# First normalization in two token halves instead of four quarters, two-bank PSUM tiles and other operand slots: a hybrid decoder layer on one core

## The chip, the core and the metric

The kernel runs on one core of one Trainium2 chip. The metric is the device time of one execution in microseconds (us); the figure for a kernel is the median of its runs. PE is the matrix engine (PEld its weight loads), DVE the vector engine, ACT the scalar engine, POOL the GpSimd engine, SP the engine whose queue issues the transfers (DMAs).

## What is computed

One layer over 1032 tokens (1024 new ones and 8 samples) of width 1024. Cut to what matters here:

```
mix = concat(o, ys) @ w_out                      # delta-rule heads and S5 heads, one output projection
x = layernorm(DN_ALPHA * x + mix, ln1_g, ln1_b)  # the FIRST normalization, over the 1024 features of a token
h = jnp.square(jax.nn.relu(x @ w_ff1))           # MLP, 4096 hidden columns
x = layernorm(DN_ALPHA * x + h @ w_ff2, ln2_g, ln2_b)
```

All is float32. The kernel keeps that precision on PE by splitting each operand into a high part `hi` and a remainder `lo`; a product is three matmuls, hi·hi, hi·lo and lo·hi.

## The kernel before

Activations lie feature by token: `acc` is eight tiles of 128 features by 1032 tokens. `HN` is 516 tokens, a half; `CH` is 258, a quarter. PE follows program order (a manual schedule); on the other engines the framework orders the instructions. A **step** is the work of one block of 128 input features.

The stage of this change lies between the mixers and the pairs of the MLP. `out2` (L1368) does, in this order:

- It loads eight weight tiles of `w_out` to stay (`resident`, L1361), through a small buffer `wraw`, into slots of the tags L and B.
- `units(c0)` (L1377) is the projection of one quarter: eight output tiles, each 4 steps of three matmuls of 258 columns into a one-bank PSUM tile (`dense_q`, L149, lines 156 to 158), then one DVE addition into `acc` (L1381). There are six such PSUM tiles (`PX`).
- `norm` calls `layer_norm_x1` (L1083) for a quarter, four times. It is a generator: at each `yield` PE is given other work worth so many microseconds of its model (`LW`, in the function `ahead`). The parts are: sums over the eight tiles (L1091 to L1097, DVE and POOL); the mean by a matmul with `onesd` (L1103), copied by ACT (L1105); subtraction (L1110 POOL, L1112 DVE), squares on ACT, their sums (L1118, L1119); the variance by small matmuls (L1124), a power on POOL (L1127); transposes that spread it (L1131); then for each of eight tiles one scaling on DVE (L1134) and `split_b` (L1137): ACT writes `hi` (L1142), DVE writes `lo` (L1148), or ACT writes a copy (L1145) and POOL writes `lo` (L1146).
- `plain(c)` (L1409) is the first MLP product for six tiles of 128 hidden columns, for a quarter of each half (258 tokens each): per tile two weight loads of 128x512 (`load_w`, L116: a transfer, ACT `whi` L113, DVE `wlo` L114; two `wraw`, three `whi`, three `wlo` buffers), then for each half 8 steps of three matmuls, ReLU and square on ACT (L1421, L1422) into one of four `hst` buffers and a store (L1423). The work after the first quarters is interleaved by `norm` and `ahead`.
- `t_forms(acc, c)` (L1151) makes four sums and differences per feature block (`tf`, L1159 to L1165) from both halves of a quarter and splits them; it is called twice, after the fourth norm.

Then `ff1` (L1563) runs ten "pairs" of the MLP in a seven-product scheme (line 1441 is every matmul there), on the operand forms B11, B21, B22 (normalized quarters of features and tokens) and T1 to T4. `ff2` makes the second product; its operand slots are drawn one after another from `RING`. `FORMS` says in which tag (Q, B, C, L, X) each form's slots lie. A slot is 128 x 1032.

Of the kernel before, what the change touches and what calls it, by code (L numbers as in the profile page):

```python
# [38 lines left out]
PX = (6, 2)  # L39
# [11 lines left out]
LW = ((2.5, 8.25, 3.0), (3.0, 8.25, 3.0), (3.0, 8.25, 2.0), (3.0, 12.25, 3.5))  # L51
# [10 lines left out]
class Kernel:  # L62
# [53 lines left out]
    def load_w(self, src, pool=None, raws=None):  # L116
        nc = self.nc
        raw = (raws or self.wp).tile([128, 512], F32, name="wraw", tag="wraw", bufs=3 if raws else 2)
# [964 lines left out]
    def layer_norm_x1(self, acc, c0, n, put, lw):  # L1083
        nc = self.nc
        V, G = nc.vector, nc.gpsimd
        items = [acc[i][:, c0:c0 + n] for i in range(8)]

        def total(a, name):
            s = self.tmp(name, n)
            s2 = self.tmp(name + "b", n)  # L1090
            V.tensor_tensor(s, a[0], a[1], op=OP.add)  # L1091
            G.tensor_tensor(s2, a[2], a[3], op=OP.add)
            V.tensor_tensor(s, s, a[4], op=OP.add)
            V.tensor_tensor(s, s, a[5], op=OP.add)
            G.tensor_tensor(s2, s2, a[6], op=OP.add)
            V.tensor_tensor(s, s, a[7], op=OP.add)
            V.tensor_tensor(s, s, s2, op=OP.add)  # L1097
            return s

        tot = total(items, "lns")  # L1100
# [3 lines left out]
        ms = self.tmp("lnsb", n)  # L1104
        nc.scalar.activation(ms, mean, AF.Copy)  # L1105
        acc2 = [self.tmp("lnq%d" % j, n, bufs=1) for j in range(2)]
        for i in range(8):
            d = items[i]
            if i in LS[0]:
                G.tensor_tensor(d, d, ms, op=OP.subtract)  # L1110
            else:
                V.tensor_tensor(d, d, mean, op=OP.subtract)  # L1112
            if i < 2:
                nc.scalar.activation(acc2[i], d, AF.Square)
            else:
                q = self.tmp("lnsq", n, bufs=3)
                nc.scalar.activation(q, d, AF.Square)
                (G if i in LS[1] else V).tensor_tensor(acc2[i % 2], acc2[i % 2], q, op=OP.add)  # L1118
        V.tensor_tensor(acc2[1], acc2[1], acc2[0], op=OP.add)  # L1119
        yield lw[1]  # L1120
        m = n // 3
        pv = self.psm()[:m, 0:3]
        for j in range(3):
            nc.tensor.matmul(pv[:, j:j + 1], acc2[1][:, m * j:m * j + m], self.onesd[:, 0:1], start=True, stop=True)  # L1124
        rs = self.tmp("lnrs", 3)[:m]
        V.tensor_scalar(rs, pv, 4e-6, None, op0=OP.add)
        G.tensor_tensor(rs, rs, self.mhalf[:m].to_broadcast([m, 3]), op=OP.pow)  # L1127
        yield lw[2]
        rb = self.psm()[:, :n]
        for j in range(3):  # L1130
            nc.tensor.transpose(rb[:, m * j:m * j + m], rs[:, j:j + 1].to_broadcast([m, 128]), self.ident[:m, :m])  # L1131
        for i in range(8):
            x = items[i]
            V.scalar_tensor_tensor(x, x, self.lnp[:, 0, i:i + 1], rb, op0=OP.mult, op1=OP.mult)  # L1134
            self.split_b(x, put[i], self.lnp[:, 1, i:i + 1], i not in LS[2])

    def split_b(self, x, dst, b, pool):  # L1137
# [5 lines left out]
        if pool:  # L1143
            t = self.tmp("lnsq", CH, bufs=3)
# [5 lines left out]
    def t_forms(self, acc, c):  # L1150
        nc = self.nc  # L1151
        V, G = nc.vector, nc.gpsimd
        h = [slice(HN * j + CH * c, HN * j + CH * c + CH) for j in range(2)]
        F = {t: self.form(t, c) for t in ("T1", "T2", "T3", "T4")}
        for i in range(4):
            a11, a12 = acc[i][:, h[0]], acc[i][:, h[1]]
            a21, a22 = acc[4 + i][:, h[0]], acc[4 + i][:, h[1]]
            t = [self.tmp("tf%d" % j, CH, bufs=1) for j in range(4)]
# [7 lines left out]
            self.split_b(t[3], F["T4"][i], None, i in TP[3])  # L1166
# [165 lines left out]
    def form(self, t, c):  # L1332
        s = [self.x1slot("x" + t, FORMS[t][c]) for _ in range(2)]
        seg = lambda j: s[j // 4][:, CH * (j % 4):CH * (j % 4) + CH]
        self.fm[t, c] = [(seg(2 * i), seg(2 * i + 1)) for i in range(4)]
        return self.fm[t, c]
# [24 lines left out]
    def resident(self, src, slots, raws=None):  # L1361
        ws = []
        for n_ in range(8):
            z = slots[n_]
            ws.append([self.load_w(src[n_], pool=(z[:, 0:512], z[:, 512:1024]), raws=raws)])
        return ws

    def out2(self, mixo, acc):  # L1368
# [6 lines left out]
        ws = self.resident(self.a["wout"][0], [self.x1slot("wr", w) for w in "LLLLLLBB"], self.tp)  # L1375

        def units(c0):  # L1377
            for n_ in range(8):
                ps = self.mmps(CH)
                yield from self.dense_q(ws[n_], mixo, c0, CH, ps)  # L1380
                V.tensor_tensor(acc[n_][:, c0:c0 + CH], acc[n_][:, c0:c0 + CH], ps, op=OP.add)  # L1381
                yield 3 * CH / 2400.0

        def norm(c, half, fill):
            put = (self.form("B11", c) + self.form("B21", c)) if not half else (self.form("B12", c) + self.form("B22", c))
            for wait in self.layer_norm_x1(acc, HN * half + CH * c, CH, put, LW[2 * c + half]):
                self.ahead(fill, wait)

        order = [(0, 0), (0, 1), (1, 0), (1, 1)]
# [546 lines left out]
```

## Time and profile before

| | |
|---|---|
| median of 3 runs | 1266.06 us (1263.64 to 1267.84) |
| the profiled execution | 1262.84 us; its span 1260.7 us; 2.1 us lie around the span |
| instructions | 25210 |
| PE busy | 1205.4 us, 96% of the span |
| DVE, ACT, POOL busy | 811.1, 637.3, 497.4 us |
| granted PE clock, mean | 0.982 |
| the stage of the change in the trace | from 491.94 us (first matmul of `out2`) to 630.93 us (first matmul of the pairs) |

Times in the rows are from the span's start. A busy time on PE includes time at a lowered clock. The releaser that a row names is the instruction whose end came last before the waiting one started.

### The profile page before, as it was taken

How to read it: one execution, taken by the hardware profiler on the slowest of the kernel's cores; microseconds unless marked ns; L12 is line 12 of the kernel's file. 1: busy time of each engine (PE TensorE's matmuls, PEld its weight loads, DVE VectorE, ACT ScalarE, POOL GpSimd, SP SyncE). 2: the span in 40 equal slices, each digit the busy share in tenths (PEclk: the TensorE clock that was granted, in tenths of full speed). 3: DMA queues.
4: the chain of work that ended last, by engine and by line, in shares of the span. 5: the costliest groups of instructions: out<-in, count | busy, mean ns of one | idle time of the engine just before them, and what ended most of it. 6: DMA issues, size and time to landing. Idle time of an engine off the chain costs nothing.

```text
span 1260.7 us, 25210 instructions
## 1 busy us (share of the span) xinstructions
PE 1205.4 (96%) x9268; PEld 1177.4 (93%) x9268; DVE 811.1 (64%) x1716; ACT 637.3 (51%) x1450; POOL 497.4 (39%) x533
## 2 busy tenths in 40 slices
PE   8999999899899899989999999999999999999996
PEld 7999999889899899988999999999999999999996
DVE  6476887788636894877745554454566575666667
ACT  5376677663646751357655555555552434352301
POOL 6243333362113660544433233323433636365214
PEclk9999999999979899999999999999999999999999
DMA  7223223122611263013446556545963646453202
GB/s 211 98 81 93 70 70 79 43 51 95 211 56 42 54 195 114 1 52 106 147 173 220 211 194 210 185 177 178 317 199 93 192 124 181 135 174 108 66 35 102
DMA packets 117995, 162.16 MB, mean 129 GB/s; under 512 B 31192, under 2 KB 70632, under 8 KB 117872
## 3 DMA queue, kind: packets, MB, share of 16 engines
q1 hardware_dynamic: 117872, 160.55, 40.5%
q8 instruction: 73, 1.20, 0.4%
q14 instruction: 50, 0.41, 0.1%
HBM read 109.94 MB, written 49.38 MB: 126 GB/s over the span
## 4 chain that ended last, share of the span: by engine, by line
PE 74%; DVE 13%; DMA 5%; ACT 3%; issue 3%; POOL 2%; SPq 0%; POOLq 0%; DVEq 0%; ACTq 0%
PE sb L1441 37%; PE mm L156 7%; PE mm L158 7%; PE mm L157 7%; DMA hst<-ht 1%; PE mm L1741 1%; DMA xraw<-in_xT 1%; DVE xB L1148 1%; DMA hst<-hd 1%; PE mm L1742 1%; PE mm L1743 1%; DVE acc L1134 1%; DVE wlo L114 1%; DMA hraw<-hd 1%; DVE cx L305 1%
## 5 line engine op out<-in xcount | busy, mean ns | idle before, releaser
L114 POOL TENSOR_TENSOR wlo<-wraw,whi 128x512 fp32r<-128x512 f32 (+1 forms) x88 | 109.1, 1241 | 188.6 <-ACT whi L113 167.9
L113 ACT ACTIVATE whi<-wraw 128x512 fp32r<-128x512 f32 (+1 forms) x164 | 100.3, 611 | 146.6 <-PE sb L1441 83.6
L1441 PE MATMUL sb<-t,whi 128*128 128x258 f32 x1008 | 162.5, 284 | 5.5 <-ACT whi L113 3.7
L1441 PEld LDWEIGHTS sb<-t,whi 128*128 128x128 f32 x1008 | 138.6, 190 | 6.7 <-ACT whi L113 4.3
L1441 PE MATMUL sb<-xT,whi 128*128 128x258 f32 x832 | 133.8, 282 | 0.0
L156 PE MATMUL mm<-xhi,whi 128*128 128x344 f32 x384 | 126.1, 328 | 0.9 <-ACT sraw L297 0.5
L157 PE MATMUL mm<-xlo,whi 128*128 128x344 f32 x384 | 123.8, 322 | 0.0
L158 PE MATMUL mm<-xhi,wlo 128*128 128x344 f32 x384 | 123.8, 322 | 0.0
L1695 DVE TENSOR_TENSOR acc<-acc,sb 128x516 f32<-128x516 f32 x112 | 76.5, 688 | 66.5 <-PE sb L1441 66.0
L1441 PEld LDWEIGHTS sb<-xT,whi 128*128 128x128 f32 x832 | 114.0, 189 | 0.0
L1441 PE MATMUL sb<-t,wlo 128*128 128x258 f32 x504 | 100.7, 283 | 0.1
L1441 PE MATMUL sb<-xB,whi 128*128 128x258 f32 x624 | 100.2, 282 | 0.0
L1441 PEld LDWEIGHTS sb<-xB,whi 128*128 128x128 f32 x624 | 85.6, 189 | 0.0
L1441 PE MATMUL sb<-xT,wlo 128*128 128x258 f32 x416 | 83.5, 282 | 0.0
L113 ACT ACTIVATE t<-hst 128x516 fp32r<-128x516 f32 x84 | 52.3, 632 | 51.6 <-DMA hst<-hd 23.9
L1441 PEld LDWEIGHTS sb<-t,wlo 128*128 128x128 f32 x504 | 77.8, 189 | 0.6 <-POOL wlo L114 0.3
L114 DVE TENSOR_TENSOR wlo<-wraw,whi 128x512 fp32r<-128x512 f32 (+1 forms) x76 | 57.1, 752 | 27.4 <-ACT whi L113 26.9
L156 PEld LDWEIGHTS mm<-xhi,whi 128*128 128x128 f32 x384 | 72.3, 188 | 2.2 <-ACT sraw L297 1.1
L157 PEld LDWEIGHTS mm<-xlo,whi 128*128 128x128 f32 x384 | 72.3, 188 | 0.4 <-issue 0.4
L158 PEld LDWEIGHTS mm<-xhi,wlo 128*128 128x128 f32 x384 | 72.2, 188 | 0.4 <-issue 0.4
L1484 DVE TENSOR_TENSOR hst<-sb,hst 128x516 f32<-128x516 f32 x40 | 27.6, 693 | 58.7 <-PE sb L1441 55.1
L114 POOL TENSOR_TENSOR t<-hst,t 128x516 fp32r<-128x516 f32 x36 | 51.4, 1437 | 32.5 <-ACT t L113 30.2
(512 smaller groups left out, 3528.8 us busy)
## 6 DMA issues: line engine op xcount, KB each, us to landing
hd<-hst SPq DMA_DIRECT2D x52, 258.0 KB
wpair<-in_wff SPq DMA_DIRECT2D x26, 512.0 KB
ht<-hsum SPq DMA_DIRECT2D x48, 258.0 KB
hst<-ht SPq DMA_DIRECT2D x48, 258.0 KB
w2raw<-in_wff SPq DMA_DIRECT2D x57, 192.0 KB
wraw<-in_win SPq DMA_DIRECT2D x40, 256.0 KB
hst<-hd SPq DMA_DIRECT2D x36, 258.0 KB
wraw<-in_wff SPq DMA_DIRECT2D x32, 256.0 KB
```

What stands on the lines that cost most here:

```text
L113: nc.scalar.activation(hi, src, AF.Copy)
L114: (lo_eng or nc.vector).tensor_tensor(lo, src, hi.bitcast(F32), op=OP.subtract)
L156: nc.tensor.matmul(ps, hi[:, k % 4, :], mh, start=(k == 0), stop=False)
L157: nc.tensor.matmul(ps, hi[:, k % 4, :], ml, start=False, stop=False)
L158: nc.tensor.matmul(ps, lo[:, k % 4, :], mh, start=False, stop=(k == last))
L305: nc.vector.scalar_tensor_tensor(out, raw[:, j:j + NP], cw[:, t, j:j + 1], out, op0=OP.mult, op1=OP.add)
L1134: V.scalar_tensor_tensor(x, x, self.lnp[:, 0, i:i + 1], rb, op0=OP.mult, op1=OP.mult)
L1148: nc.vector.scalar_tensor_tensor(lo, x, b, hi.bitcast(F32), op0=OP.add, op1=OP.subtract)
L1441: self.nc.tensor.matmul(ps[:, 512 * c:512 * c + CH], a[:, k, :], forms[c][k][b], start=(start and k == 0 and a is hi and b == 0), stop=(st ...
L1484: V.tensor_tensor(h3, self.banks(ps), h3, op=OP.add)
L1695: V.tensor_tensor(a, a, self.banks(ps), op=OP.add)
L1741: nc.tensor.matmul(ps, hi[:, k % 4, :], mh, start=(k == 0), stop=False)
```

## The change

The first normalization works on 516 tokens at a time, two blocks instead of four. The projection and the plain tiles work on halves as well: `units(half)` and `plain(half)` have one two-bank PSUM tile for 516 tokens and `dense_h`, whose step is six matmuls of 258 columns. `PX` becomes three two-bank tiles and one two-bank tile `st`, which serves mean, variance and spread scale of a block in turn. The plain tiles run all of the first half, then all of the second; the weights are still loaded twice. `t_forms` handles 516 tokens, cycles seven temporaries that the normalization used, yields to PE after each feature block, and writes the last two blocks of T4 after the plain tiles. Each form has one slot per feature block that holds `hi` and `lo` of 516 tokens, and `FORMS` and `RING` name other tags in another order. The weights of the projection pass through the temporaries `lnsq`. Cut to the core:

```diff
-RING = "XXLLLLLLQBQBQBQBQBQBQBQQCQCQQB"
+RING = "XXQQQQBBBBBBBBLLLLQQQQQQQQLLCC"
-FORMS = {"B11": "QL", "B21": "QL", "B12": "XX", "B22": "CL", "T1": "BQ", "T2": "BQ", "T3": "BQ", "T4": "BQ"}
+FORMS = {"B11": "BBBB", "B21": "QQQQ", "B12": "CCXX", "B22": "LLLL", "T1": "BBBB", "T2": "QQQQ", "T3": "QQQQ", "T4": "LLCC"}
-PX = (6, 2)
+PX = (3, 1)
-LW = ((2.5, 8.25, 3.0), (3.0, 8.25, 3.0), (3.0, 8.25, 2.0), (3.0, 12.25, 3.5))
+LW = ((3.0, 11.0, 3.0), (3.0, 13.0, 3.5))
+TW = 9.0
+TMPS = ("tf0", "tf1", "lns", "lnq0", "lnq1", "lnsb", "lnsb")
...
+    def layer_norm_half(self, acc, half, put, lw):
+        items = [acc[i][:, HN * half:HN * half + HN] for i in range(8)]
...
         yield lw[0]
-        mean = self.psm()[:, :n]
-        nc.tensor.matmul(mean, self.onesd, tot, start=True, stop=True)
+        st = self.sm.tile([128, 1024], F32, name="st", tag="sm")
+        mean = self.banks(st)
+        for c in range(2):
+            nc.tensor.matmul(mean[:, c, :], self.onesd, s[:, CH * c:CH * c + CH], start=True, stop=True)
...
         yield lw[1]
-        m = n // 3
-        pv = self.psm()[:m, 0:3]
-        for j in range(3):
+        m = CH // 3
+        pv = st[:m, 300:306]
+        for j in range(6):
...
         yield lw[2]
-        rb = self.psm()[:, :n]
-        for j in range(3):
+        for j in range(6):
+            nc.tensor.transpose(mean[:, j // 3, ...], rs[:, j:j + 1].to_broadcast([m, 128]), self.ident[:m, :m])
         for i in range(8):
+            x = self.halves(items[i])
+            V.scalar_tensor_tensor(x, x, self.lnp[:, 0, i:i + 1], mean, op0=OP.mult, op1=OP.mult)
+            self.split_b(items[i], put[i], self.lnp[:, 1, i:i + 1], i not in LS[2])
...
+    def dense_h(self, w, mov, h0, ps):
+        last = 4 * len(w) - 1
+        for k in range(last + 1):
+            hi, lo = w[k // 4]
+            for j, (a, b) in enumerate(((hi, 0), (hi, 1), (lo, 0))):
+                for c in range(2):
+                    self.nc.tensor.matmul(ps[:, 512 * c:512 * c + CH], a[:, k % 4, :],
+                                          mov[k][b][:, h0 + CH * c:h0 + CH * c + CH], ...)
+            if k < last:
+                yield 6 * CH / 2400.0
...
-        order = [(0, 0), (0, 1), (1, 0), (1, 1)]
...
-        norm(1, 1, first)
-        if TO == 2:
-            self.t_forms(acc, 0)
-        self.t_forms(acc, 1)
-        self.ahead(first, 999)
-        self.ahead(self.plain(1), 999)
+        self.ahead(units(0), 99)
+        rest = units(1)
+        norm(0, rest)
+        self.ahead(rest, 99)
+        rest = (x for half in range(2) for x in self.plain(half))
+        norm(1, rest)
+        for wait in self.t_forms(acc):
+            self.ahead(rest, wait)
+        self.ahead(rest, 999)
```

## Rows read from the trace of the kernel before

**Rows 1.** The page of the whole execution: busy time, share of the span and instructions of each engine; then the chain of work that ended last, by engine.

```profile
PE 1205.4 (96%) x9268; PEld 1177.4 (93%) x9268; DVE 811.1 (64%) x1716; ACT 637.3 (51%) x1450; POOL 497.4 (39%) x533
...
PE 74%; DVE 13%; DMA 5%; ACT 3%; issue 3%; POOL 2%; SPq 0%; POOLq 0%; DVEq 0%; ACTq 0%
```

**Rows 2.** Windows: from:to, the length, then busy time and instructions of PE, PEld, DVE, ACT and POOL, the granted PE clock, the DMA share and GB/s.

```profile
491.90:631.10 139.20, 127.65 (x1008) 124.90 (x1007) 106.95 (x210) 74.99 (x191) 63.91 (x75) 0.96 0.23 73
...
542.90:631.10 88.20, 79.01 (x602) 76.55 (x601) 69.33 (x123) 61.85 (x158) 43.68 (x50) 0.94 0.36 112
...
550.00:560.00 10.00, 6.40 (x41) 6.19 (x40) 8.78 (x16) 5.61 (x16) 5.34 (x7) 0.83 0.23 69
...
590.00:600.00 10.00, 7.97 (x51) 7.39 (x50) 9.96 (x17) 8.55 (x22) 6.24 (x7) 0.83 0.16 54
...
620.00:630.00 10.00, 10.00 (x74) 10.00 (x73) 4.39 (x8) 5.49 (x15) 2.56 (x3) 0.83 0.69 210
```

**Rows 3.** Waits of PE: who waited for whom, us in total, times, longest. The first three rows are of the stage (491.9 to 631.1), the last is the largest of the rest of the execution (631.1 to 1260.7).

```profile
PE mm L158 <- DVE wlo L114: 6.6, 4, 3.6
PE mm L157 <- DVE xB L1148: 2.5, 4, 1.8
PE ps L1124 <- DVE lnq L1119: 2.4, 1, 2.4
...
PE sb L1441 <- ACT whi L113: 3.7, 3, 2.0
```

**Rows 4.** PE in order of time: start, duration, line, output and inputs, shape, count, and in brackets the idle time before and its releaser. They are the first matmul of the stage; the mean, the variance and the spread of the first quarter, each with the second matmul behind it; the first plain matmul; the matmul after the longest wait; the first matmul of the pairs.

```profile
491.94 0.28 PE L156 MATMUL mm<-moh,wr 128*128 128x258 f32 x1
...
506.31 0.60 PE L1103 MATMUL ps<-lns,onesd 128*128 128x258 f32 x2
...
506.86 0.28 PE L157 MATMUL mm<-mol,wr 128*128 128x258 f32 x1
...
516.09 0.55 PE L1124 MATMUL ps<-onesd,lnq 128*86 128x1 f32 x6
...
516.70 0.28 PE L157 MATMUL mm<-mol,wr 128*128 128x258 f32 x1
...
520.18 0.39 PE L1131 MATMUL ps<-ident,lnrs 86*128 86x86 f32 x3
...
520.57 0.28 PE L157 MATMUL mm<-mol,wr 128*128 128x258 f32 x1
...
542.92 0.28 PE L156 MATMUL mm<-xB,whi 128*128 128x258 f32 x1
...
555.82 0.41 PE L158 MATMUL mm<-xB,wlo 128*128 128x258 f32 x1 [3.60 <-DVE wlo L114]
...
630.93 0.63 PE L1441 MATMUL sb<-xB,whi 128*128 128x258 f32 x4
```

**Rows 5.** DVE in order of time, columns as in the rows above: the last addition of a projection quarter and the last of its sums; the eight scalings of the first quarter and the first `lo` behind them.

```profile
503.61 0.42 DVE L1381 TENSOR_TENSOR acc<-acc,mm 128x258 f32<-128x258 f32 x1 [1.01 <-PE mm L158]
...
504.60 0.43 DVE L1097 TENSOR_TENSOR lns<-lns,lnsb 128x258 f32<-128x258 f32 x1
...
520.73 3.24 DVE L1134 SCALAR_TENSOR_TENSOR acc<-acc,lnp,ps 128x258 f32<-128x258 f32 x8
523.88 0.98 DVE L1148 SCALAR_TENSOR_TENSOR xB<-acc,lnp,xB 128x258 fp32r<-128x258 f32 x1
```

**Rows 6.** Groups of DVE instructions: line, names, shapes, count, busy us and mean ns of one, idle time before and its releasers. The first is of the page (the same addition on 516 columns, in the second product); the others are of the stage.

```profile
L1695 DVE TENSOR_TENSOR acc<-acc,sb 128x516 f32<-128x516 f32 x112 | 76.5, 688 | 66.5 <-PE sb L1441 66.0
...
L114 DVE TENSOR_TENSOR wlo<-wraw,whi 128x512 fp32r<-128x512 f32 x23 | 20.0, 872 | 10.6 <-ACT whi L113 10.6
L1148 DVE SCALAR_TENSOR_TENSOR xB<-acc,lnp,xB 128x258 fp32r<-128x258 f32 x20 | 15.3, 810 | 0.0
L1381 DVE TENSOR_TENSOR acc<-acc,mm 128x258 f32<-128x258 f32 x32 | 13.3, 418 | 11.9 <-PE mm L158 11.9
...
L1161 DVE TENSOR_TENSOR tf<-acc,tf 128x258 f32<-128x258 f32 x8 | 5.6, 700 | 0.3
L1165 DVE TENSOR_TENSOR tf<-acc,tf 128x258 f32<-128x258 f32 x8 | 5.3, 661 | 0.7 <-POOL xT L114 0.6
L114 DVE TENSOR_TENSOR xT<-tf,xT 128x258 fp32r<-128x258 f32 x10 | 5.0, 518 | 0.5 <-ACT xT L113 0.5
L1159 DVE TENSOR_TENSOR tf<-acc 128x258 f32<-128x258 f32 x8 | 5.0, 622 | 0.6 <-POOL xT L114 0.6
L1148 DVE SCALAR_TENSOR_TENSOR xT<-tf,lnbd,xT 128x258 fp32r<-128x258 f32 x6 | 3.3, 555 | 0.3 <-ACT xT L1142 0.3
```

**Rows 7.** Groups of POOL instructions, columns as in rows 6: two of the normalization and its `lo` at 258 columns, then a subtraction of 516 columns from the second product.

```profile
L1110 POOL TENSOR_TENSOR acc<-acc,lnsb 128x258 f32<-128x258 f32 x16 | 12.5, 815 | 3.9 <-ACT lnsb L1105 3.9
L1146 POOL TENSOR_TENSOR xB<-lnsq,xB 128x258 fp32r<-128x258 f32 x12 | 10.9, 913 | 19.2 <-ACT lnsq L1145 19.1
L1118 POOL TENSOR_TENSOR lnq<-lnq,lnsq 128x258 f32<-128x258 f32 x12 | 10.5, 872 | 3.8 <-ACT lnsq L1117 3.6
...
L114 POOL TENSOR_TENSOR t<-hst,t 128x516 fp32r<-128x516 f32 x36 | 51.4, 1437 | 32.5 <-ACT t L113 30.2 <-PE sb L1441 2.1
```

**Rows 8.** SP's queue in order of time: the first weight transfer after those fetched ahead for the plain tiles, and the first transfer for the pairs.

```profile
555.79 0.33 SPq L119 DMA_DIRECT2D wraw<-in_wff  x1
...
623.53 0.92 SPq L1461 DMA_DIRECT2D wpair<-in_wff  x2
```

More of the change, by code (lines that the diff above doesn't have):

```diff
@@ L1148, in split_b, with t_forms @@
             nc.vector.scalar_tensor_tensor(lo, x, b, hi.bitcast(F32), op0=OP.add, op1=OP.subtract)
-    def t_forms(self, acc, c):
+    def t_forms(self, acc):
         nc = self.nc
         V, G = nc.vector, nc.gpsimd
-        h = [slice(HN * j + CH * c, HN * j + CH * c + CH) for j in range(2)]
-        F = {t: self.form(t, c) for t in ("T1", "T2", "T3", "T4")}
+        F = {t: self.form(t) for t in ("T1", "T2", "T3")}
+        F["T4"] = []
+        h = [slice(HN * j, HN * j + HN) for j in range(2)]
+        last = []
         for i in range(4):
@@ L1165, in t_forms @@
             V.tensor_tensor(t[3], a21, t[1], op=OP.subtract)
[L1166 removed]
+            last.append(t[3])
+            if i < 2:
+                F["T4"].append(self.piece("T4", i))
+                self.split_b(t[3], F["T4"][i], None, i in TP[3])
+            yield TW if i < 3 else 999
+        for i in range(2, 4):
+            F["T4"].append(self.piece("T4", i))
+            self.split_b(last[i], F["T4"][i], None, i in TP[3])
+        self.form_views("T4", F["T4"])
     def weave(self, main, filler, per_us, per_stage=0.0):
@@ L1384, in norm @@
-        def norm(c, half, fill):
-            put = (self.form("B11", c) + self.form("B21", c)) if not half else (self.form("B12", c) + self.form("B22", c))
-            for wait in self.layer_norm_x1(acc, HN * half + CH * c, CH, put, LW[2 * c + half]):
-                self.ahead(fill, wait)
-        order = [(0, 0), (0, 1), (1, 0), (1, 1)]
-        us = [units(HN * half + CH * c) for c, half in order]
-        self.ahead(us[0], 99)
-        chain = lambda *gs: (x for g in gs for x in g)
-        norm(0, 0, chain(us[1], us[2]))
@@ L1394, in out2 @@
-        self.ahead(us[1], 99)
-        norm(0, 1, chain(us[2], us[3]))
-        self.ahead(us[2], 99)
-        if TO == 0:
-            self.t_forms(acc, 0)
-        first = self.plain(0)
-        norm(1, 0, chain(us[3], first))
-        self.ahead(us[3], 99)
-        if TO == 1:
-            self.t_forms(acc, 0)
-        norm(1, 1, first)
-        if TO == 2:
-            self.t_forms(acc, 0)
-        self.t_forms(acc, 1)
-        self.ahead(first, 999)
-        self.ahead(self.plain(1), 999)
@@ L1411, in plain, with norm @@
-    def plain(self, c):
+                ps = self.mmh()
+                yield from self.dense_h(ws[n_], mixo, HN * half, ps)
+                a = self.halves(acc[n_][:, HN * half:HN * half + HN])
+                V.tensor_tensor(a, a, self.banks(ps), op=OP.add)
+                yield 6 * CH / 2400.0
+        def norm(half, fill):
+            put = self.form("B1%d" % (half + 1)) + self.form("B2%d" % (half + 1))
+            for wait in self.layer_norm_half(acc, half, put, LW[half]):
+                self.ahead(fill, wait)
@@ L1412, in plain @@
+        self.ahead(units(0), 99)
[7 more added lines that the diff above has]
+        self.ahead(rest, 999)
+    def plain(self, half):
         nc = self.nc
-        mov = [self.fm["B1%d" % (h + 1), c] + self.fm["B2%d" % (h + 1), c] for h in range(2)]
+        mov = self.fm["B1%d" % (half + 1)] + self.fm["B2%d" % (half + 1)]
@@ L1416, in plain @@
             w = self.load_w8(self.a["wff1"][f])
-            for half in range(2):
-                ps = self.mmps(CH)
-                yield from self.dense_q(w, mov[half], 0, CH, ps)
-                h = self.hst()[:, :CH]
-                nc.scalar.activation(h, ps, AF.Relu)
-                nc.scalar.activation(h, h, AF.Square)
-                nc.sync.dma_start(self.hd[f][:, HN * half + CH * c:HN * half + CH * c + CH], h)
-                yield 3 * CH / 2400.0
+            ps = self.mmh()
+            yield from self.dense_h(w, mov, 0, ps)
+            h = self.hst()
+            nc.scalar.activation(self.halves(h), self.banks(ps), AF.Relu)
+            nc.scalar.activation(h, h, AF.Square)
+            nc.sync.dma_start(self.hd[f][:, HN * half:HN * half + HN], h)
+            yield 6 * CH / 2400.0
     def bank(self):
```

89 lines of the change are left out of this document (45 added, 44 removed).

## The prediction

> **What bounds the kernel now.** The page comes first: PE is busy 96% of the span and makes up 74% of the chain that ended last [rows 1]. A change that leaves PE's work alone can only win back time in which PE waits or runs at a lowered clock, so the next views are PE's waits and the windows. The stage of the change lasts 630.93 - 491.94 = 139.0 us [rows 4]. From its first matmul to the first mean lie 120 matmuls (96 of a quarter and 8 steps of three), so one takes (506.31 - 491.94) / 120 = 0.1198 us [rows 4]; a step of six takes 0.719. The stage has 384 + 576 = 960 of them: 115.0 us. A norm adds 0.43 for the mean, 0.49 for the variance and 0.27 for the spread, each from its start to the second matmul behind it, less one matmul [rows 4]; four norms make 4.8. PE's own work is therefore 119.8 us, and 19.2 us are lost. Of these 11.5 are waits: 6.6 for the weight remainders `wlo`, 2.5 for `lo` parts of the normalized operands, 2.4 for a sum of squares, all of them DVE's [rows 3]. The clock is the next part: three windows of 10 us show 0.83 [rows 2], that is some 3.4 us at 1.2 GHz in place of 2.4, and half of this, 1.7, is lost each time. Each of the three follows a wait, as the longest one of 3.60 us [rows 4]. 2.6 us are left for restarts.
>
> Behind it stands DVE: 106.95 us busy in 139.2, and 69.33 of 88.2 from the first plain matmul on [rows 2], where every wait but one lies. So the question is when DVE's work falls due.
>
> **The change, step by step.** *PE's work* stays: 192 matmuls per half of the projection, 288 per half of the plain tiles, and two norms of 0.86 + 0.98 + 0.54 make the same 4.8 us. Forecast times below count 0.719 a step.
>
> *DVE's price.* The same addition costs 418 ns on 258 columns and 688 on 516 [rows 6], so 258 more columns cost 0.27, and a merged pair saves 0.15 at most; eight scalings in 3.24 us are 0.405 each [rows 5], so 0.675 on 516. A `lo` took 0.81 on average, twice what the scaling of the same form does; POOL works on its own `lo` parts at the time [rows 6, 7]. No row shows 516 columns of it. Below it cannot be cheaper than the scaling, 0.675; above, it waits for one whole POOL instruction, 1.44 on 516 [rows 7], so 2.1. I take the nearest row scaled like the scaling, 0.81 x 0.675 / 0.405 = 1.35.
>
> *First norm.* The first half of the projection ends at 491.94 + 32 x 0.719 = 514.9. Three DVE instructions, in before 1.4 us from the last addition to the last sum's end [rows 5], take 2.2 and end at 517.4; PE asks after 5 steps, at 518.5. After the mean (519.4) seven POOL instructions of 1.44 and about 1.7 for ACT and the last DVE sum make 11.8; PE asks after 18 steps, 12.9 us. Both are covered. The spread is done at 537.4, and 4 of 32 steps remain, until 540.3. Here the cover ends. In the rows eight scalings run first and the `lo` parts behind them [rows 5], so DVE scales until 537.5 + 8 x 0.675 = 542.9 and the first `lo` is there at 544.2. PE has done two matmuls and waits **3.7 us**; before, three quarters were through with their `lo` parts or nearly so when the plain tiles began. The next `lo` parts, one late projection addition (0.69) among them, come at 545.6, 547.6 and 549.0, slower than PE's steps; the lowered clock that I expect after the wait lies inside this pace. The second norm's mean, due after 5 steps at 543.9, is reached at 550.2, and its sum, with two more DVE instructions of about 0.9 behind the fifth `lo` (550.3), is ready at 552.1. Mean at 552.15: **8.25 us late**, all causes together (bounds: 3.8 less with `lo` at 0.675; 3.8 more with 2.1).
>
> *Second norm.* 21 steps, 15.1 us, cover its 11.8; 6 steps cover the power. Spread done at 573.9, with 16 steps of the first half left as cover (11.5 us) for DVE's 5.4 of scalings and 6.75 of `lo`, and with three `wlo` of 0.87 [rows 6] and the first T differences in the same queue. I expect no wait for the `lo` parts but one `wlo` late by 2.0 us (mean of the four before 1.65, longest 3.6 [rows 3]) and a lowered clock after it, 1.7: **3.7 us** (bounds 0 and 5.3).
>
> *Weights.* Before, a plain weight served both halves in turn, and the second weight of the next tile had to be split in the 2.9 us between the release of a `whi` and its need. Now one is used for four steps on end, 2.9 us, and three buffers leave 5.7 us for a split of some 1.5. So the 6.6 us of `wlo` waits go, but for the one above. SP issues half as many stores, of twice the size; the weight transfer that before stood behind a store [rows 8] does so still.
>
> *T forms.* Their DVE groups sum to 24.2 us [rows 6]; at 688 / (2 x 418) per column pair that is 20. Before, the first quarters' T forms ran between the third and fourth norms' work; now all of them come after the second norm, at 579.4. From there DVE has 6.75 + 20 + 14 x 0.87 = 39 us to do in the 44 until the pairs. It fits narrowly, and the pairs' later products want the last T forms later still.
>
> *Start of the pairs.* Their first transfers went out 7.4 us ahead of their first matmul [rows 4, 8], and PE did not wait. Two temporaries of T4's last blocks now stay busy to the end; if they held the room of the first transfer, up to those 7.4 us would come bare. Only two of four buffers are needed first, so I put 0.5, for PSUM banks and T1 too.
>
> *Second product.* The ring has the same 30 slots, each index one slot; the first plain forms now take slots whose last use is the last pair's first or third product, not its fourth. Nothing changes on the path: PE's waits there are small (the largest group 3.7 [rows 3]). I allow 2 us either way for shifted timing.
>
> **Sum.** 573.9 + 64 steps (46.0) + 3.7 + 0.5 = 624.1 against 630.93: 6.8 us less. The profiled execution gives 1262.84 - 6.8 = 1256.0; it is 3.2 below the median of the runs, so the forecast for the median is 1266.06 - 6.8 = **1259.3 us**.
>
> **Rivals.** A, *no late queue*: `lo` at 0.675 (for it: DVE and POOL seldom need the same moment in the longer instructions; against: every norm's rows show the mean of 0.81). Mean at 548.35, 3.8 earlier, and no second wait, another 3.7: 14.3 less, 1251.8 us.
>
> B, *each `lo` is held for a whole POOL instruction*, 2.1 us. The mean of 0.81 at 258 is 0.4 more than the scaling, half of POOL's 0.91 [rows 6, 7], which speaks for half a hold, not a whole one. The second mean comes 3.8 later, the rest as forecast: 3.0 less, 1263.1 us, which is no change that can be told. The Trainium skill ("SBUF — State Buffer", section "Who interferes with whom") says that a DVE instruction with two SBUF inputs and a reading GpSimd instruction exclude each other for the whole instruction; by that rule longer POOL instructions speak against this change. By its rule the sum would be B's 1263.1, by the row 1259.3.
>
> C, *slower: DVE is the bound from the second norm on.* The hold of B also falls on the T forms: (6.75 + 20) x 2.1 / 1.35 + 12.2 = 53.8 us from 579.4, so to 633.2; the last `wlo` lies at the end of that queue with one weight's 2.9 us of PE behind it, less the about 2 us of T work that may follow it: pairs at 634.1, 3.2 later, and 1.0 for T1: 4.2 more, 1270.3 us. It decides from the point at which DVE's work after 579.4 exceeds PE's 44 us. For it: DVE is 9.96 busy of 10 in the window at 590 before [rows 2]. Against it: T forms may run on into the pairs, where DVE has room.
>
> That the edit fails to do what it says can be left out: tile widths and order are fixed in the code.
>
> **How the numbers follow.** Forecast 0.44, A 0.21, B 0.18, C 0.17. About 0.3% (3.8 us) is what a measurement of this kernel can tell from no change: faster means below 1262.3, slower above 1269.9. The forecast's own spread (1255 to 1263, from the second wait's bounds and the 2 us of the second product) lies nearly all in faster, A wholly, a little of B: 0.62. Same takes most of B and a share of C: 0.22. Slower is the rest of C: 0.16. The range leaves out the ends of A and C: 1250 to 1268.5.
>
> **What would show it.** Right: the first plain matmul at about 540, with a wait of 3 to 4 us behind its first two, for `lo`; a second mean at 551 to 553; spread of the second at 573 to 575; `wlo` waits of PE of 3 us at most in place of 6.6; one or two windows at a lowered clock in place of three; DVE up to 9 us less busy in the stage (some 60 merged pairs of 0.15); the pairs at 622 to 626. Wrong, if PE waits for a sum of squares (POOL longer than 1.44 each), if plain matmuls wait for T work or for PSUM evacuation, if the first pair's transfers come after the last plain matmul, or if the time after the first pair differs by more than 2 us.

## The result and the profile after

The changed kernel takes 1273.12 us (median of 6 runs, 1270.45 to 1276.03), the kernel before in the same comparison 1264.04 (6 runs): ratio 1.0085, 95% interval 1.0067 to 1.0104 (the quotient of the two medians is 1.0072). It is slower by 9 us; the forecast was 6.8 us faster. The profiled execution took 1274.95 us (span 1273.2), 12.1 more than that of before. In the experiments below, one run of the changed kernel "without T, `lo` one scaling behind" and one of before beside it lie apart at a far lower granted clock (0.748 and 0.653) and are left out.

First, as for before, the page's busy times of the changed kernel:

```profile
PE 1211.9 (95%) x9268; PEld 1182.9 (93%) x9268; DVE 807.9 (63%) x1625; ACT 625.5 (49%) x1366; POOL 493.3 (39%) x496
```

DVE is less busy than before [rows 1], and 91 instructions fewer. The averages look better and the time is worse. The waits of PE in the stage, 491.69 to 638.86, tell more (who waited for whom: us in total, times, longest):

```profile
PE mm L1363 <- DVE wlo L116: 9.8, 5, 4.9
PE mm L1363 <- DVE xB L1149: 4.5, 2, 3.8
PE sb L1464 <- ACT whi L115: 1.2, 1, 1.2
PE st L1125 <- DVE lnq L1120: 0.9, 1, 0.9
PE mm L1363 <- DVE acc L1390: 0.9, 1, 0.9
```

The stage is 147.2 us, 8.2 longer than before. The `wlo` waits, which the forecast had all but removed, went from 6.6 [rows 3] to 9.8; the `lo` waits from 2.5 to 4.5; those for a sum of squares fell from 2.4 to 0.9. PE in order of time (start, duration, what, and in brackets the idle time before and its releaser): the first variance, the first plain matmuls with the forecast wait, the second mean, the second spread and the matmul behind it, then the `wlo` waits of the first four tiles that had any, and the first pair.

```profile
533.55 1.08 PE L1125 MATMUL st<-onesd,lnq 128*86 128x1 f32 x12 [0.91 <-DVE lnq L1120]
...
543.08 0.41 PE L1363 MATMUL mm<-xB,whi 128*128 128x258 f32 x2
547.25 0.51 PE L1363 MATMUL mm<-xB,whi 128*128 128x258 f32 x2 [3.76 <-DVE xB L1149]
...
554.26 1.46 PE L1104 MATMUL st<-lns,onesd 128*128 128x258 f32 x4
...
576.02 0.61 PE L1131 MATMUL st<-ident,lnrs 86*128 86x86 f32 x6
576.42 0.73 PE L1363 MATMUL mm<-xB,whi 128*128 128x258 f32 x4
...
590.70 0.80 PE L1363 MATMUL mm<-xB,wlo 128*128 128x258 f32 x2 [4.85 <-DVE wlo L116]
596.58 0.51 PE L1363 MATMUL mm<-xB,wlo 128*128 128x258 f32 x2 [0.36 <-DVE wlo L116]
601.23 0.51 PE L1363 MATMUL mm<-xB,wlo 128*128 128x258 f32 x2 [1.49 <-DVE wlo L116]
606.74 0.80 PE L1363 MATMUL mm<-xB,wlo 128*128 128x258 f32 x2 [2.37 <-DVE wlo L116]
...
638.86 0.74 PE L1464 MATMUL sb<-xB,whi 128*128 128x258 f32 x4 [1.21 <-ACT whi L115]
```

The second spread is done at 576.42, when the next matmul starts. That is 84.7 us after the first matmul of the stage, 2.8 us behind the forecast (82.0); from there to the pairs it takes 62.4 against 50.2. So 12.2 of the 15 us lie behind the second norm. What stood in DVE's queue there (same columns; x8 is eight instructions in one row):

```profile
576.66 5.39 DVE L1135 SCALAR_TENSOR_TENSOR acc<-acc,lnp,st 128x516 f32<-128x516 f32 x8 [2.22 <-PE st L1131]
581.97 0.68 DVE L116 TENSOR_TENSOR wlo<-wraw,whi 128x512 fp32r<-128x512 f32 x1
582.57 0.69 DVE L1162 TENSOR_TENSOR tf<-acc 128x516 f32<-128x516 f32 x1
583.18 0.69 DVE L1162 TENSOR_TENSOR lnq<-acc 128x516 f32<-128x516 f32 x1
583.79 5.18 DVE L1149 SCALAR_TENSOR_TENSOR xB<-acc,lnp,xB 128x516 fp32r<-128x516 f32 x3
588.90 1.75 DVE L116 TENSOR_TENSOR wlo<-wraw,whi 128x512 fp32r<-128x512 f32 x1
```

The `whi` of the last row was ready at 580.1 (ACT, 0.61 us from 579.52). Its remainder started 8.8 us later, behind T differences and three `lo` parts of 1.73 us each, and took 1.75 itself. A 516-column instruction is 0.69 here when POOL rests. What POOL did at that time:

```profile
580.21 1.31 POOL L1166 TENSOR_TENSOR lns<-acc 128x516 f32<-128x516 f32 x1 [6.47 <-DVE acc L1135]
582.07 4.66 POOL L1147 TENSOR_TENSOR xB<-lnsq,xB 128x516 fp32r<-128x516 f32 x2 [0.55 <-ACT lnsq L1146]
586.70 1.72 POOL L1166 TENSOR_TENSOR lnsb<-acc 128x516 f32<-128x516 f32 x1
588.38 1.72 POOL L1147 TENSOR_TENSOR xB<-lnsq,xB 128x516 fp32r<-128x516 f32 x1
```

The two take turns: 1.73 on DVE in place of 0.69, 1.72 on POOL in place of 1.31. Windows of 10 us (busy time and count of PE, PEld, DVE, ACT, POOL, then the granted clock):

```profile
530.00:540.00 10.00, 9.09 (x68) 8.88 (x68) 5.11 (x8) 0.00 (x0) 3.68 (x3) 0.83 0.01 2
580.00:590.00 10.00, 5.85 (x49) 5.64 (x47) 10.00 (x11) 7.64 (x14) 9.24 (x5) 0.96 0.08 26
590.00:600.00 10.00, 8.68 (x48) 8.18 (x48) 10.00 (x10) 6.48 (x12) 6.61 (x5) 0.70 0.27 79
600.00:610.00 10.00, 6.41 (x40) 6.20 (x41) 10.00 (x13) 6.89 (x12) 5.59 (x3) 0.83 0.25 81
620.00:630.00 10.00, 10.00 (x86) 10.00 (x85) 2.60 (x4) 4.67 (x8) 0.00 (x0) 1.00 0.48 157
```

DVE is full for 30 us and nearly idle in the window at 620: the T work came in a burst, long before the pairs need it. In and behind the waits the clock is lowered: at 0.96, 0.70 and 0.83 the three windows from 580 on hold 10.2 us at 1.2 GHz. For 2.0 us of them PE was still in a wait (from 589.2 to 590.7 and from 606.2 to 606.7), where the clock costs nothing; the other 8.2 us cost half, 4.1 us. With 46.0 of steps and 9.8 and 1.2 of waits that makes 61.1 of the 62.4; 1.3 are left for PE's restarts behind its waits.

### The profile page after: what moved, and what is told of

Read it like the earlier page. It is cut to its first block, busy times and chain, and to the rows that moved or that the text cites. A ratio compares the mean times of both kernels' runs of the same rounds, so it can differ in the third digit from the quotient of the medians.

```text
span 1273.2 us, 24939 instructions
## 1 busy us (share of the span) xinstructions
PE 1211.9 (95%) x9268; PEld 1182.9 (93%) x9268; DVE 807.9 (63%) x1625; ACT 625.5 (49%) x1366; POOL 493.3 (39%) x496
## 4 chain that ended last, share of the span: by engine, by line
PE 75%; DVE 10%; DMA 5%; issue 4%; ACT 3%; POOL 2%; SPq 1%; POOLq 0%; DVEq 0%; ACTq 0%
PE sb L1464 37%; PE mm L158 6%; PE mm L159 6%; PE mm L160 6%; PE mm L1363 5%; DMA hst<-ht 1%; PE mm L1764 1%; PE mm L1766 1%; PE mm L1765 1%; DMA hraw<-hd 1%; DVE t L116 1%; DVE acc L1135 1%; PE mm L145 1%; DVE xB L1149 1%; PE mm L146 1%
## 5 line engine op out<-in xcount | busy, mean ns | idle before, releaser
L116 DVE TENSOR_TENSOR wlo<-wraw,whi 128x512 fp32r<-128x512 f32 (+1 forms) x76 | 60.4, 796 | 33.8 <-ACT whi L115 31.4
L1363 PE MATMUL mm<-xB,whi 128*128 128x258 f32 x384 | 67.1, 298 | 4.5 <-DVE xB L1149 4.5
```

The lines of the kernel that those rows point to most:

```text
L116: (lo_eng or nc.vector).tensor_tensor(lo, src, hi.bitcast(F32), op=OP.subtract)
L1363: self.nc.tensor.matmul(ps[:, 512 * c:512 * c + CH], a[:, k % 4, :], mov[k][b][:, h0 + CH * c:h0 + CH * c + CH], start=(k == 0 and j == 0) ...
```

## The experiments

"After" is the changed kernel, "before" the former one. Each ratio is against runs of before on the same chip (median 1262.8 to 1263.6). The changed kernel itself ran only in the comparison above, whose interval is 2.3 us to either side; a difference to its 1273.1 is no more exact than that.

| kernel | median us | ratio to before (95%) |
|---|---|---|
| before without T | 1256.65 | 0.9942 (0.9929 to 0.9956) |
| after without T | 1259.64 | 0.9966 (0.9954 to 0.9978) |
| after, T paced | 1266.34 | 1.0021 (1.0007 to 1.0035) |
| after, POOL off | 1265.31 | 1.0015 (1.0001 to 1.0029) |
| after, only the norms' `lo` on DVE | 1272.28 | 1.0079 (1.0055 to 1.0104) |
| after, both cures | 1261.83 | 0.9985 (0.9971 to 0.9998) |
| ... and `lo` one scaling behind | 1259.73 | 0.9967 (0.9952 to 0.9982) |
| ... or one `lo` per two scalings | 1259.76 | 0.9973 (0.9958 to 0.9988) |
| after without T, `lo` one scaling behind | 1255.90 | 0.9946 (0.9929 to 0.9964) |
| before, POOL off | 1268.74 | 1.0039 (1.0024 to 1.0055) |
| before, POOL off, T paced | 1265.01 | 1.0013 (0.9999 to 1.0027) |
| after, all cures, stores on POOL's queue | 1255.94 | 0.9954 (0.9936 to 0.9971) |

My theory was that T work in front of the weight remainders, and instructions held for POOL, make the loss. The rivals: DVE's amount of work; something else in the new layout.

### Without the T forms

The T forms' operands are replaced by those of the plain tiles, in both kernels (the edit of the changed one is shown). This leaves out their work on DVE, ACT and POOL, so the results are not the layer's:

```diff
-        for wait in self.t_forms(acc):
-            self.ahead(rest, wait)
+        for t, b in (("T1", "B11"), ("T2", "B21"), ("T3", "B22"), ("T4", "B11")):
+            self.form_views(t, self.fm[b])
```

> The changed kernel without the T forms (their computation is left out; the pairs read the normalized forms in their place, as many matmuls as before). Theory 'late weights': in the changed kernel all T work falls on DVE and POOL right after the second norm, the weight remainders wait in DVE's queue behind it, and this is where the time went. Then of PE's 9.8 us of waits for wlo some 3 are left (the one behind the second norm's scalings and lo parts), with one stretch at the lower clock fewer or two: 1259 to 1263 us. Rival 'shape': the loss lies in the two-bank tiles, the single tile for the norm and the other slots; it stays without T work: 1270 us or more.

> The kernel before, likewise without the T forms. Late weights: it too loses the waits that T work causes, the one of 2.0 and two of 0.5 us for wlo and a stretch at the lower clock: 1257 to 1261 us, so that the two kernels without T forms stand within 3 us of each other. Shape: the changed one stays 8 us slower than this one.

Before without T came 0.4 us below its range, after within it. Without T the two stand 3.0 us apart, with T 9.1 (1273.1 against 1264.0). So some 6 us of the loss come with the T work and 3 do not. `wlo` waits of after fall from 9.8 to 2.6 and, what I had not expected, those of before from 6.6 [rows 3] to 1.7. T work had made most of them before, too.

### The T work in another order, or without POOL

First, the first and the third difference of each T block are pinned behind what is issued ahead of them on their engine:

```diff
+            pin = self.tc.keep_in_program_order
-            V.tensor_tensor(t[0], a12, a11, op=OP.subtract)
+            pin(V.tensor_tensor(t[0], a12, a11, op=OP.subtract))
...
-            (G if i in TE else V).tensor_tensor(t[2], a22, a12, op=OP.subtract)
+            pin((G if i in TE else V).tensor_tensor(t[2], a22, a12, op=OP.subtract))
```

> The changed kernel, with the first difference (DVE) and the third (POOL) of each feature block of the T forms pinned behind everything issued before them on their engine, so that the four blocks are spread over the plain tiles of the second half and the weight remainders pass between them. Same work. Late weights: PE's waits for wlo fall from 9.8 to 4 to 6 us (the longest, 4.9, lies among the second norm's lo parts and loses only the T differences ahead of it, about 1.3), 1267 to 1270 us. Shape: no change, 1273 us.

6.8 us of the loss came back, a little more than expected, with the same work on the same engines: `wlo` waits 4.5. DVE's busy time in the stage is nearly the same (94.6 us, 95.75 in the changed kernel), so the order alone carries most of it. Then the order is left, and POOL's part of the T forms and of the norms' `lo` goes to DVE:

```diff
-LS = ((1, 3, 4, 7), (2, 4, 6), (0, 1, 2, 3, 6))
+LS = ((1, 3, 4, 7), (2, 4, 6), (0, 1, 2, 3, 4, 5, 6, 7))
...
-TP = ((1, 3), (0, 1, 3), (0,), (2,))
+TP = ((), (), (), ())
...
-TE = (0, 1, 2, 3)
+TE = ()
```

> The changed kernel with all T work and all lo parts of the normalization on DVE, none on POOL (three lo parts per norm and eleven instructions of the T forms move). Theory 'hold': a DVE instruction with two inputs in SBUF costs 1.7 us instead of 0.68 while POOL works, so DVE gets faster by more than the moved work: lo parts at 0.68, the second mean at 551 to 552 instead of 554.3, waits for wlo 4 to 6 us instead of 9.8, 1264 to 1268 us. Rival 'amount': DVE is simply full there, and the 17 moved instructions of 0.6 us add 10 us to it: 1277 us or more.

DVE got 17 instructions more and its busy time in the stage fell from 95.75 to 90.87 us. That is the amount rival's end. (ACT loses ten copies by the edit, too; but the `whi` above was ready 8.8 us ahead of its remainder, so ACT was not what held that one up.) DVE of this kernel in order of time, from the second norm's scalings on:

```profile
574.67 5.39 DVE L1135 SCALAR_TENSOR_TENSOR acc<-acc,lnp,st 128x516 f32<-128x516 f32 x8 [1.88 <-PE st L1131]
579.97 0.68 DVE L116 TENSOR_TENSOR wlo<-wraw,whi 128x512 fp32r<-128x512 f32 x1
580.57 0.69 DVE L1162 TENSOR_TENSOR tf<-acc 128x516 f32<-128x516 f32 x1
581.18 0.69 DVE L1162 TENSOR_TENSOR lnq<-acc 128x516 f32<-128x516 f32 x1
581.79 2.08 DVE L1149 SCALAR_TENSOR_TENSOR xB<-acc,lnp,xB 128x516 fp32r<-128x516 f32 x3
583.79 0.69 DVE L1166 TENSOR_TENSOR lns<-acc 128x516 f32<-128x516 f32 x1
584.39 0.68 DVE L116 TENSOR_TENSOR wlo<-wraw,whi 128x512 fp32r<-128x512 f32 x1
```

It is the same beginning as above, but three `lo` take 2.08 in place of 5.18 and the second `wlo` ends 5.1 us after the first began, not 8.7. To see whether the norms' part or the T forms' part of POOL's work mattered, only `LS` was changed, `TP` and `TE` left:

> The changed kernel with only the norms' three lo parts each moved from GpSimd to DVE; the T forms stay as they are, with their work on both engines. Theory 'the T forms' hold is what costs': the second mean moves from 554.3 to about 552.6, the waits for weight remainders stay at 7 to 10 us, and the time is 1270 to 1273 us, at most 2 to 3 under the changed kernel's 1273.1. Rival 'the norm's lo parts' (most of what the kernel without GpSimd won, 7.8 us, came from them): waits of 5 us, 1265 to 1268.

As the theory had it: second mean at 552.34, `wlo` 9.4, 1272.3. The mean came true by luck: of the 1.9 us by which it comes earlier after the stage's start, 1.5 were won before the first spread, which the edit does not touch (a lowered clock behind the first variance that this execution did not have). The time is 0.8 us under the changed kernel's, which the intervals cannot tell from nothing. So POOL's `lo` parts of the norms cost little, and that its T work cost the other 7 follows by subtraction; it was not tried alone. Now both cures, pinned order and POOL off:

> The changed kernel with both cures at once: GpSimd does none of the lo parts and differences of the norm's last step and of the T forms, and the first and third difference of each T block are pinned behind what is issued before them on their engine. Alone, the first gave 1265.3 us with 5.1 us of waits for weight remainders left, the second 1266.3 with 4.5. Theory 'two prices' (the T work in front of the remainders, and instructions held for GpSimd, are separate parts of the loss): those last waits fall to 2 us or less, and the clock lost behind them comes back: 1258 to 1262 us. Rival 'one price' (both cures take away the same wait): 1264 to 1267. Rival 'amount' (on a DVE that does all the work, pinned T work comes due too late for the pairs): a wait of over 4 us at the first pair, 1266 to 1270.

1261.8: 11.3 of the loss back, `wlo` 1.7. The two prices add up for the most part, and the changed kernel no longer loses against before.

### The same on the kernel before

> The former kernel with GpSimd's lo parts and differences (12 of the norms, 14 and 8 of the T forms, 258 columns each) moved to DVE. Theory 'hold' (a DVE instruction with two SBUF inputs waits for a working GpSimd wherever they meet): DVE gets 34 instructions of about 0.42 us more, 14 us, and wins back about 0.4 us on each of some 30 that meet GpSimd now; waits for weight remainders fall from 6.6 to about 4: 1258 to 1262 us against 1263.4. Rival 'long instructions' (the hold costs time only with 516 columns): within 1.5 us of 1263.4. Rival 'amount' (14 us more on DVE count whole where PE waits for it): 1266 to 1270.

My theory failed here: 5.2 us slower, though the `wlo` waits fell from 6.6 to 0.6. Its waits of PE in the stage:

```profile
PE ps L1124 <- DVE lnq L1119: 10.4, 2, 6.6
PE mm L157 <- DVE xB L1148: 2.4, 4, 1.6
PE mm L158 <- DVE wlo L114: 0.6, 2, 0.4
```

The 6.6 lie at the third norm, where T work now stood ahead of the sum of squares in DVE's queue; the other 3.8 at the second, ahead of any T work (2.4 in the kernel before [rows 3]). With the T differences pinned, as above:

> The former kernel with GpSimd's 34 instructions on DVE, which took 1268.7 us and waited 10.4 us for sums of squares behind T differences, and with the first and third difference of each T block pinned behind what is issued before them. Theory 'what stands in front' (not DVE's amount, but T work ahead of what PE waits for made it slow): the waits for sums of squares fall to 3 us or less, those for remainders rise to some 3 us, and the time is 1259 to 1263 us, no slower than the former kernel's 1263.5. Rival 'amount': the same waits turn up at the remainders, 1266 to 1270.

1265.0, between the theories. The sum-of-squares waits fell to 4.6, not to 3: the one at the third norm to 0.9, the one at the second stayed at 3.8, as there is no T work in front of it. And 6.2 us turned up at the first pair, which waited for a split weight. So the hold was not what limited before, and taking POOL out is no gain where the order then puts other work in front.

### The 3 us that are not T

In the next one, on top of both cures, each `lo` follows one scaling behind, pinned; the scalings from the second on are pinned as well:

```diff
-            V.scalar_tensor_tensor(x, x, self.lnp[:, 0, i:i + 1], mean, op0=OP.mult, op1=OP.mult)
-            self.split_b(items[i], put[i], self.lnp[:, 1, i:i + 1], i not in LS[2])
+            s = V.scalar_tensor_tensor(x, x, self.lnp[:, 0, i:i + 1], mean, op0=OP.mult, op1=OP.mult)
+            if i:
+                self.tc.keep_in_program_order(s)
+            nc.scalar.activation(put[i][0], items[i], AF.Identity, bias=self.lnp[:, 1, i:i + 1])
+            for j in [i - 1] * (i > 0) + [7] * (i == 7):
+                self.tc.keep_in_program_order(V.scalar_tensor_tensor(
+                    put[j][1], items[j], self.lnp[:, 1, j:j + 1], put[j][0].bitcast(F32), op0=OP.add, op1=OP.subtract))
```

> As the one with both cures, and in each norm's last step the lo parts follow one scaling behind, pinned, instead of behind all eight scalings. If the 3 us by which the changed kernel without T forms stands above the former one are the first wait of the plain matmuls (3.8 us, 3.1 with GpSimd off): the first lo part is there about 1.5 us after the spread, the wait shrinks to under 1 us, the second mean comes at about 549.5 to 550.5 instead of 552.6, and the time is 2 to 3 us under the kernel with both cures: 1256 to 1259. Rival 'DVE's sum' (the mean needs the same scalings, lo parts and sums in whatever order): the wait is spread over several steps, the mean moves by under 1 us, and so does the time.

2.1 us less, as large as expected at its lower end (the time itself misses its range by 0.7), but not in the expected way: the second mean came only 1.1 us earlier after the stage's start. The wait of 3.1 in one piece became three of 0.95 and one of 1.93. The lowered clock became less, but most of all it came later. The windows 541 to 551 and 551 to 561 of the kernel with both cures, then of this one:

```profile
541.00:551.00 10.00, 6.85 (x39) 6.64 (x38) 10.00 (x16) 5.33 (x9) 0.46 (x1) 0.72 0.00 0
551.00:561.00 10.00, 9.16 (x68) 8.84 (x68) 7.48 (x10) 5.30 (x10) 5.97 (x5) 0.94 0.11 33
```

```profile
541.00:551.00 10.00, 7.16 (x52) 6.25 (x51) 9.87 (x16) 4.82 (x7) 1.31 (x1) 1.00 0.00 0
551.00:561.00 10.00, 8.07 (x51) 7.58 (x50) 7.81 (x11) 6.44 (x12) 5.22 (x4) 0.83 0.07 26
```

When the second spread is done, nothing is won yet: 82.9 us after the stage's start, 82.4 in the kernel with both cures. What this kernel wins in these two executions, 3.6 us, lies behind it. There the kernel with both cures had one more wait, 1.7 us, and 1.7 us of lowered clock behind it:

```profile
589.06 0.51 PE L1364 MATMUL mm<-xB,wlo 128*128 128x258 f32 x2 [1.72 <-DVE wlo L116]
```

Here it is gone: in the new order remainders pass DVE between the scalings. The 1.93 was the mean waiting for the last scaling of the first norm, as both use the one PSUM tile `st`:

```profile
553.07 1.56 PE L1104 MATMUL st<-lns,onesd 128*128 128x258 f32 x3 [1.93 <-DVE acc L1135]
```

With one `lo` after each two scalings (`[i // 2] * (i % 2) + [4, 5, 6, 7] * (i == 7)`) that scaling ends earlier:

> As the kernel with both cures and the lo parts one scaling behind (1259.7 us, where the second mean waited 1.9 us for the last scaling of the first norm, which reads the same PSUM tile), but with one lo part after each two scalings, and the last four behind. The last scaling ends about 2 us earlier. Theory 'the shared PSUM tile': the mean no longer waits for the scaling and comes about 1.5 us earlier after the spread (11.5 instead of 13.0 us), 1257.5 to 1259.5 us. Rival 'DVE's sum' (sums of the mean are now what is late): the mean moves by less than 0.7 us and the time stays at 1259 to 1261.

The rival held. The mean now waited 1.45 for its own sums and came 13.7 us after the spread (13.0 before); the time is the same. It is the sum of DVE's work there, not the PSUM tile. And without T, all `lo` on DVE, one scaling behind:

> The changed kernel without the T forms' work (their operands are those of the plain tiles, so the results differ), all lo parts of the norms on DVE, each one scaling behind. Without T the changed kernel took 1259.6 us and the former one 1256.65. If those 3 us are the first wait of the plain matmuls (3.8 us in one piece, and the lowered clock behind it), this one takes 1256 to 1258. Rival 'elsewhere' (slots, PSUM, the second norm): 1259 to 1260.5, with the wait spread and nothing won.

1255.9 against 1256.65 of before without T: the 3 us come with the norms' `lo` parts, their order and POOL's share in them together, as this kernel changes both. The place is not the expected one. From the end of the first spread to that of the second, where the first plain matmuls lie, this kernel takes 36.0 us, after without T 36.5; from there to the pairs 47.3 against 51.7. In after without T three `lo` parts of 1.74 us stood there in front of a remainder, PE waited for it, and 1.7 us of lowered clock followed (the row of DVE, then that of PE):

```profile
581.60 5.21 DVE L1149 SCALAR_TENSOR_TENSOR xB<-acc,lnp,xB 128x516 fp32r<-128x516 f32 x3
```

```profile
587.47 0.51 PE L1363 MATMUL mm<-xB,wlo 128*128 128x258 f32 x2 [2.55 <-DVE wlo L116]
```

In this kernel that wait is gone.

### The start of the pairs

The second product's first addition comes 315.8 us after the pairs' first matmul, before the change 313.9: 2 us more are lost there in these two executions. SP's queue in the changed kernel (`x2` spans the time from the first to the last of the group):

```profile
627.75 5.80 SPq L1446 DMA_DIRECT2D hd<-hst  x2
633.65 2.76 SPq L1484 DMA_DIRECT2D wpair<-in_wff  x4
```

The first pair's transfers go out 5.2 us ahead of the pairs (7.4 before), right behind a store that waited for ACT's square of a tile. In the kernel with `lo` one scaling behind, the first 10 us of the pairs run like this:

```profile
624.53:634.53 10.00, 10.00 (x70) 9.99 (x71) 5.42 (x6) 3.97 (x7) 5.57 (x4) 0.83 0.34 118
```

So the six stores of the second half were put on POOL's queue:

```diff
-            nc.sync.dma_start(self.hd[f][:, HN * half:HN * half + HN], h)
+            (nc.gpsimd if half else nc.sync).dma_start(self.hd[f][:, HN * half:HN * half + HN], h)
```

> As the kernel with both cures and the lo parts one scaling behind (1259.7 us), with the six stores of the second half's plain tiles issued on GpSimd's queue, which has nothing else there. Up to now the first pair's four weight transfers stand in SyncE's queue behind a store that waits for the square of the last tile but one; they went out 5.7 us ahead of the first pair in place of 7.4, PE waited 1.7 us for the first split weight, and the clock fell behind that wait (the first 10 us of the pairs at 0.83). Theory 'the store in front': the transfers go out at least 7 us ahead, the wait is under 0.5 us, the window stays at 1.00, and the time is 2.5 to 4 us less: 1255.5 to 1257.5. Rival 'the room' (the last T4 temporaries hold the room of these transfers until they are split in the last tile): the transfers go out as late as before and the time stays within 1 us of 1259.7. Rival 'more traffic' (stores and loads now at the same time): the weights of the last plain tiles come late, 1260 to 1262.

SP and PE of this kernel:

```profile
610.47 9.22 SPq L1490 DMA_DIRECT2D wpair<-in_wff  x4
```

```profile
622.77 0.75 PE L1470 MATMUL sb<-xB,whi 128*128 128x258 f32 x4 [1.21 <-ACT whi L115]
```

The first transfer went out 12.3 us ahead, and the first 10 us of the pairs are at 1.00. The median is 3.8 us lower, as much as was expected, but the two come from different comparisons: by the ratios to before, 0.9967 and 0.9954, it is 1.6 us, and the intervals overlap. The traces show 1.7 us of clock and 0.5 of wait won. The wait was to go as well; it fell from 1.7 to 1.2, which is what it is in the changed kernel. The reason stands in ACT's rows of the same kernel: the split waits its turn behind the last tile's ReLU, not for its weight.

```profile
621.60 0.60 ACT L1450 ACTIVATE hst<-mm 128x516 f32<-128x516 f32 x1 [3.44 <-PE mm L1369]
622.09 0.62 ACT L115 ACTIVATE whi<-wpair 128x512 fp32r<-128x512 f32 x1
```

This kernel beats both: 0.9954 of before (0.9936 to 0.9971). That is not what the change alone is worth: this order of the `lo` parts and this place of the stores were not tried on the kernel before.

## Why the prediction was wrong

The step that failed is the one behind the second norm. "Weights" had the `wlo` waits go, "T forms" had the T work fit, and so 3.7 us of one wait and its clock were forecast there. The trace shows 9.8 us of waits for `wlo` and 4.1 us of clock: remainders stood in DVE's queue behind T work and behind `lo` parts that took turns with POOL. One by one:

**First norm.** Right in mechanism and nearly in size: a wait of 3.76 at the first plain matmuls (3.7 forecast), for the named reason. The price of a `lo` came true as a mean only: the ten of both norms took 1.37 on average (1.35 forecast), but single ones 0.74 to 1.77; the first two took 1.54, the next three 0.84. "Both are covered" was wrong by 0.9 us for the sum of squares: POOL's additions for it took 1.73 each, not 1.44. The clock of 0.83 that follows costs 1.7 more, and with it the spread was done at 540.10 in place of 537.4. These 1.7 belong to the execution and not to the change: of the nine traces of the changed kernel's variants, all with the same wait, eight have no lowered clock behind it. The mean was 554.26 against 552.15. It did not wait for its sum, as forecast (that was done at 553.3): PE came to it late, after 2.7 us lost to a lowered clock that the forecast had put inside DVE's pace. So the size of this lateness is in part luck.

**Second norm.** From its mean to the end of its spread 22.2 us (21.75 forecast). The 3.7 us for one late `wlo` were the failure, together with the next two steps.

**Weights.** "The 6.6 us of `wlo` waits go" rested on the time between the release of a `whi` buffer and its need. Before without T waits 1.7: buffers never were the main cause. T work was, and in the changed kernel more of it stood ahead of the remainders in DVE's queue, as the rows above show.

**T forms.** "It fits narrowly" compared amounts, 39 us in 44. The amount fitted: DVE had 7 us of 10 free at 620. But a T difference needs nothing except `acc` and is ready as soon as the scaling is; nothing holds it back until the pairs, so it ran ahead of remainders that PE was about to need. Pinning it gave 6.8 us. And at 1.7 to 1.8 us in place of 0.69 while POOL worked, each instruction in front cost two and a half times as much: another 4.5 us with both cures (1266.3 to 1261.8).

**Start of the pairs.** 0.5 forecast; 1.2 of wait and some 2 behind it. Of the weight transfer that stood behind a store the prediction says that it "does so still", and it does not price this: the transfers went out 5.2 us ahead of the pairs, not 7.4. But the store is not what made the 1.2: with the stores moved and the transfers out 12.3 us ahead the wait was the same, behind ACT's ReLU, which the forecast had not counted.

**Second product.** The sign of being wrong that the prediction names, more than 2 us of difference after the first pair, is there in the two profiled executions: 634.3 us from the pairs' first matmul to the end of the span against 629.8. 1.9 of these 4.6 us are those at the start of the pairs. Behind them the changed kernel's trace has two stretches at a lowered clock, 1.7 us each, 373 and 458 us after the first pair's matmul; before has none, but before without T has two as well, so they are no mark of the change. The medians differ by 9.1, the stage and the pairs' start by 10.2.

**The rivals.** C had the side, and 1270.3 of 1273.1, but by another way, so that it came near is in part luck. Its hold on the T forms is there, in rows. Its reason, DVE's work exceeding PE's 44 us, is not: DVE was busy for 44.3 us of the 62.8 from the start of the second spread to the pairs, and 17 instructions more on it made the kernel 7.8 us faster. What C lacked is the order. The rule quoted for B (the Trainium skill, "SBUF — State Buffer", "Who interferes with whom": a DVE instruction with two SBUF inputs and a reading GpSimd instruction exclude each other) agrees with the trace in the main: both engines alternate at 1.72 to 1.75 us. That is a little less than a whole hold, which with 0.69 and 1.31 would be 2.00; here the measurement counts.

## What to carry to other kernels

A queue's amount of work against the time until it is due tells whether it can fit, not whether it does: for each instruction that PE waits for, ask what is ready earlier in the same queue with a later due time. When blocks are merged, work that used to be spread between them becomes one such burst; pin it behind the urgent work, and price every instruction of it at its contended duration. Stores that become larger become later, and hold up the loads that are issued behind them in the same queue. And a gain in the expected size can lie in another place than the expected one: compare the two traces stretch by stretch before you believe the reason.

## What the runs showed of the hardware

Moving work from an engine to its neighbour lowered the neighbour's busy time: DVE 95.75 to 90.87 us with 17 instructions more.

How long a wait was does not tell whether a lowered clock followed. One and the same wait of 0.9 us at the first variance was followed by 1.2 GHz in the changed kernel and in after without T, at a cost of 1.7 us, and in the eight other variants of it by none. Nor did it help by itself to cut a wait into pieces: behind 3.1 us in one piece the kernel with both cures lost 3.1 us to the clock, with pieces of 0.95 and 1.93 1.7 us were lost, and with pieces of 0.67, 1.60, 1.00 and 1.45 us (one `lo` per two scalings) the clock was at 1.2 GHz from 548.0 to 558.3 and 4.3 us were lost.
